# Merge stage in program order: where the norms' activation table is asked for, how wide the late norms work, and which engine makes the first weight sums

## Chip, cores and metric

The kernel runs on one core of one Trainium2 chip. The metric is device time in microseconds for one execution. The kernel before takes 3202.3 us, the median of three runs from 3200.66 to 3202.62 us.

Engines are called by their names in the profile: PE is TensorE (matmuls; PEld are its weight loads), DVE is VectorE, ACT is ScalarE, POOL is GpSimd, and SP is the engine whose queue issues most DMAs.

## What is computed

One encoder layer over 2048 prompt tokens and 32 new tokens, width 1024, in fp32. Cut to what matters here:

```python
h = rmsnorm(x, g_pre_mix) * (1 + scale_m) + shift_m
z = h @ w_in                                    # feeds two mixers and two gates
ya = band_attention(...);  yb = gla(...)
merged = sigmoid(gate_a) * (ya @ w_br_a) + sigmoid(gate_b) * (yb @ w_br_b)
x = x + gate_m * rmsnorm(merged @ w_out, g_post_mix)

h = rmsnorm(x, g_pre_ffn) * (1 + scale_f) + shift_f
u = h @ w_up                                    # 1024 -> 5632
yf = (gelu(conv3(u)[:2816]) * conv3(u)[2816:]) @ w_down
x = x + gate_f * rmsnorm(yf, g_post_ffn)
```

`rmsnorm` needs 1/sqrt(mean(x*x) + eps) for each token.

## The kernel before

**Number format.** Each fp32 factor of a product is split into a high part (an ACT copy that rounds) and a low part (a DVE subtraction), and each product is three matmuls: high by high, high by low, low by high.

**Layout.** Activations lie transposed: channels on the 128 partitions, in eight tiles `m` = 0 to 7, tokens along the row. The 2080 tokens are cut into eight blocks `b` of 260 columns.

**Merge stage (about 1480 to 1781 us of the profile).** For each block four `merge` steps form two tiles each of the merged branches, and eight `project` steps multiply by `w_out`. `begin()` and `end()` bracket a slot, one such step. What the other engines do for a slot is put into a plan by slot and rank (`at(slot, rank, f)`) and written out by `flush`. From line 1218 all five engines are in program order: the order of the text is the order of each queue, so an instruction that waits holds everything behind it on its engine.

**The planned norms.** `norm_plan` does blocks 0 to 5 wholly and the first norm of block 6: thirteen norms. `share` takes the sum of squares (`sa1` after the projection, `sa2` before the feed-forward), splits it (ACT L1317, DVE L1320) and sums it over the partitions with two matmuls by ones (PE L1324, L1325). Two slots on, `rstd_of` makes 1/sqrt: ACT `Ln` (L1332), ACT `Exp` (L1333), and a Newton step of three DVE operations (L1334 to L1336). `ln_exp_table()` (L105) asks for the activation table that holds both functions. It is called at line 1221, where the stage in program order begins, and not in `rstd_of`. The stage's remaining ACT functions are Copy, Square and Identity.

**The late norms.** Blocks 6 and 7 are finished while the feed-forward runs, by the generator `norms(b)`, which starts in the second column of token pair 1 (`hold`). It goes one step further in each `side()`, of which a column has seven. It works by single tiles of 128x260: for each of eight `m` a multiplication, a step later an addition of x, a step later a square, two steps per tile; then the second norm; then for each `m` a multiplication, the shift on ACT a step later, and a store to `h2T` a step later, one step per tile. `rstd_late` calls `ln_exp_table()` itself (L1418). It hands two matmuls to the next column's start and goes on in that column's sixth step.

**Who waits for the late norms.** `ndone` counts blocks whose `h2T` is stored. `sums(2)` builds the operand sums of token pair 2 from `h2T` and stores them in `hT`; it waits for `ndone` = 8. `load_ops` fetches the operands of pair 2 (ACT L1719, DVE L1720) from column 18 of pair 1 on. When both generators have ended, `s3` is closed and its space becomes two more weight buffers and one more place in the ring of split weights.

**Feed-forward.** The products run as seven half-size products in place of eight (a Strassen-like scheme), for three pairs of token segments. `UNITS[0]` to `UNITS[2]` are the up-projection of the three pairs with 22 columns each; one column is seven products of twelve matmuls (L1868). For pair 0 the sums of weight quarters (S1 to S4) are made and stored to `sW`; pairs 1 and 2 read them back. `total3` makes S1, S2, S3 with three operations of 128x512 (L1779): on POOL for unit 0, on DVE for the first units of the down-projection. S4 is on DVE in all of them. The splits of weights are ACT L1805 and DVE L1810, their loads SP L1775, the stores of the sums SP L1813.

Of the kernel before, what the change touches and what calls it, by code (L numbers as in the profile page):

```python
# [13 lines left out]
AF = mybir.ActivationFunctionType  # L14
# [6 lines left out]
KD = 8  # L21
# [10 lines left out]
ND = 260  # L32
# [7 lines left out]
def dap(ap, offset, dims):  # L40
    return bass.AP(tensor=ap.tensor, offset=ap.offset + offset, ap=dims)
# [6 lines left out]
def parts(c0, n):  # L48

    out = []  # L50
    if c0 < TP:
        out.append((0, min(n, TP - c0), 0))
    if c0 + n > TP:
        out.append((max(0, TP - c0), n, 1))
    return out
# [3 lines left out]
def encoder_step(ctx: ExitStack, tc: tile.TileContext, I, O):  # L59
    nc = tc.nc  # L60
# [44 lines left out]
    def ln_exp_table():  # L105
        i = nc.scalar.preload_act_table_set("natural_log_exp_and_others")
        if not in_order[0]:
            tc.keep_in_program_order(i)
# [14 lines left out]
    h2T = dram.tile([D, T], F32, name="h2T")  # L123
# [114 lines left out]
    with ExitStack() as st:  # L238
# [178 lines left out]
        for s_ in range(2, 10):  # L417
            b = s_ // 2
# [799 lines left out]
    ordered.enter_context(tc.manual_schedule(engines={getattr(mybir.EngineType, x) for x in  # L1218
                                                      ("PE", "Activation", "DVE", "Pool", "SP")}))
    in_order[0] = True  # L1220
    ln_exp_table()

    MH = [(area(fA[0], 9232, KD, ND), area(fA[1], 8192, KD, ND)),
          (area(mhl, 0, KD, ND), area(mhl, KD * ND, KD, ND))]
    o_ = [d3.tile([128, KD, ND], F32, name=f"o{x}") for x in range(2)]
    sa1, sa2, sqE, sqR, h2 = [d3.tile([128, 2, ND], F32, name=x) for x in ("sa1", "sa2", "sqE", "sqR", "h2")]
# [3 lines left out]
    def two(dt):  # L1230
        return [d3.tile([128, ND], dt, name=x, tag=x) for x in ("sh", "sl")]
# [15 lines left out]
    def rows2(src, j, b):  # L1247
        return dap(src, 256 * j * T + ND * b, [[T, 128], [128 * T, 2], [1, ND]])
# [62 lines left out]
    def share(b, slot, sa, r):  # L1311
# [15 lines left out]

        after_pe[slot + 1] = total

    def rstd_of(q, r):  # L1330
        r0, t = two(F32)
        nc.scalar.activation(r0, q, AF.Ln, bias=eps, scale=1.0 / D)  # L1332
        nc.scalar.activation(r0, r0, AF.Exp, scale=-0.5)  # L1333
        nc.vector.scalar_tensor_tensor(t, q, D * EPS, r0, op0=OP.add, op1=OP.mult)  # L1334
        nc.vector.scalar_tensor_tensor(t, t, -0.5 / D, r0, op0=OP.mult, op1=OP.mult)
        nc.vector.scalar_tensor_tensor(r, t, 1.5, r0, op0=OP.add, op1=OP.mult)  # L1336
# [3 lines left out]
    def over2(r):  # L1340
        return r.unsqueeze(1).to_broadcast([128, 2, ND])
# [9 lines left out]
    def squares(b, j, s):  # L1351
        nc.scalar.activation(s, o_[b % 2][:, 2 * j:2 * j + 2], AF.Square)

    def x1_store(b, j):
        nc.sync.dma_start(rows2(x1T, j, b), o_[b % 2][:, 2 * j:2 * j + 2])

    def shift(b, x, m):
        for a, e, s in parts(ND * b, ND):
            nc.scalar.activation(x[:, a:e], x[:, a:e], AF.Identity, bias=mod[:, 3, m, s:s + 1],
                                 scale=mod[:, 4, m, s:s + 1])  # L1360
# [86 lines left out]
    def soon(n, f):  # L1447

        later(n - 1, f) if in_order[0] else f()

    def norms(b):

        o, t0, xl = o_[b % 2], ND * b, (h2, sqR)

        def square(m):
            nc.scalar.activation((sa2 if m < 2 else sqE)[:, m % 2], o[:, m], AF.Square)
            if m % 2:
                x1_store(b, m // 2)
                if m > 1:
                    soon(1, lambda: nc.vector.tensor_add(sa2, sa2, sqE))  # L1460

        def add(m):
            nc.vector.tensor_add(o[:, m], o[:, m], xl[m // 2 % 2][:, m % 2])
            soon(1, lambda: square(m))

        def modulate(m):
            nc.vector.tensor_mul(o[:, m], o[:, m], r)

            def store():
                nc.sync.dma_start(h2T[128 * m:128 * m + 128, t0:t0 + ND], o[:, m])  # L1470
                if m == KD - 1:
                    ndone[0] += 1

            def late():
                shift(b, o[:, m], m)
                soon(1, store)

            soon(1, late)

        while hold[0]:  # L1480
            yield
        for j in range(2):
            nc.sync.dma_start(xl[j], rows2(I["xT"], j, b))
        yield
        yield
        r = rs1
        if b == NBLK - 1:
            yield from rstd_late(sa1[:, 0])
        for m in range(KD):
            nc.vector.tensor_mul(o[:, m], o[:, m], r)  # L1490
            soon(1, lambda m=m: add(m))
            yield
            yield
            if m in (1, 3):
                nc.sync.dma_start(xl[m // 2], rows2(I["xT"], 2 + m // 2, b))
        yield
        yield
        pair_sum(sa2)
        yield
        yield  # L1500
        r = yield from rstd_late(sa2[:, 0])
        for m in range(KD):
            modulate(m)
            yield

    NBLK = T // ND
# [1 line left out]
    ndone = [0]  # L1508
# [251 lines left out]
    def weights():  # L1760


        cols = [(u, m) for u in range(len(UNITS)) for m in range(NM[u])]
        fresh = [UNITS[u][0] == 0 for u, m in cols]
        todo = [(c, x) for c in range(len(cols)) for x in (("A21", "A22", "A11", "A12") if fresh[c] else WOPS)]
        at = {}
        born = {}
        cur = -1

        def fetch():  # L1770
            while todo and free and todo[0][0] <= cur + 1:
                c, x = todo.pop(0)
                at[c, x] = i = free.pop(0)
                born[c, x] = tick[0]
                nc.sync.dma_start(raw(i, NK[cols[c][0]]), w_rows(*cols[c], x))  # L1775

        def total(c, eng, op, out, a, b):
            n = NK[cols[c][0]]
            getattr(eng, op)(raw(out, n), raw(a, n), raw(b, n))  # L1779

        def total3(c):
            at[c, "S1"] = s1 = free.pop(0)
            s2, a21 = free.pop(0), at.pop((c, "A21"))
            born.update({(c, x): tick[0] + 1 for x in ("S1", "S2", "S3")})
            eng = nc.vector if cols[c][0] else nc.gpsimd
            a11, a22 = at[c, "A11"], at[c, "A22"]
            total(c, eng, "tensor_add", s1, a21, a22)

            def others():
                total(c, eng, "tensor_sub", s2, s1, a11)  # L1790
                total(c, eng, "tensor_sub", a21, a11, a21)
                at[c, "S2"], at[c, "S3"] = s2, a21

            soon(1, others)

        def part(c, x, i):
            u, m = cols[c]
            while True:
                place = ring((u, m, x))
                if place:  # L1800
                    break
                yield
            n = NK[u]
            hi, lo = place
            act = nc.scalar.activation(hi[:, :n], raw(i, n), AF.Copy)  # L1805
            if not in_order[0]:
                tc.keep_in_program_order(act)

            def low():
                nc.vector.tensor_sub(lo[:, :n], raw(i, n), f32(hi[:, :n]))  # L1810
                WO[u, m, x] = place
                if fresh[c] and x in SUM:
                    nc.sync.dma_start(w_rows(u, m, x), raw(i, n))  # L1813
                if fresh[c] and x == "A12":

                    def total4():
                        total(c, nc.vector, "tensor_sub", i, i, at[c, "S2"])
                        at[c, "S4"] = i

                    soon(1, total4)  # L1820
                elif fresh[c] and x == "S2":
                    soon(4, lambda: free.append(at.pop((c, "S2"))))
                else:
                    soon(3 if fresh[c] and x in SUM else 1, lambda: free.append(i))

            soon(1, low)

        fetch()
        yield
        for cur in range(len(cols)):  # L1830
            for x in SPLITS if fresh[cur] else WOPS:
                if fresh[cur] and (cur, "S1") not in at and x == SPLITS[0]:
                    while len(free) < 2:
                        yield
                    total3(cur)
                if x == "A22" and cur + 1 < len(cols) and fresh[cur + 1] and len(free) > 1 \
                        and all((cur + 1, y) in at for y in ("A21", "A22", "A11")):
                    total3(cur + 1)
                while (cur, x) not in at:
                    fetch()  # L1840
                    if (cur, x) not in at:
                        yield
                while in_order[0] and cur < 5 and tick[0] < born.get((cur, x), -9) + 2:

                    yield
                i = at[cur, x]
                if not (fresh[cur] and x == "S2"):
                    del at[cur, x]
                yield from part(cur, x, i)
                yield  # L1850
                fetch()
# [471 lines left out]
```

## Time and profile before

| | |
|---|---|
| profiled execution | 3196.12 us |
| its span | 3194.4 us |
| median of three runs | 3202.3 us |
| PE busy | 3066.6 us (96%) |
| DVE busy | 2240.5 us (70%) |
| ACT busy | 1682.3 us (53%) |
| POOL busy | 373.5 us (12%) |
| mean TensorE clock granted | 0.988 |

A group's row in the profile gives line, engine, operation, tiles written and read, shape, count, then busy time and mean duration in ns, then the idle time of the engine just before and what ended it. In rows in order of time the first number is the start in us, the second the duration, and the bracket holds the engine's idle time before and the releaser. Rows of windows give the busy time and the number of instructions of each engine, the granted clock, the DMA share and GB/s. Rows of waits give total us, number of times, longest.

### The profile page before, as it was taken

What the parts mean: (1) busy time and instruction counts of PE and PEld (TensorE: products, weight loads), DVE (VectorE), ACT (ScalarE), POOL (GpSimd) and SP (SyncE); (2) the same over time, 40 slices, a digit from 0 to 9 for tenths busy, and PEclk for the clock granted to TensorE, in tenths of its full rate; (3) what the DMA queues carried; (4) which work ended last, traced back from release to release, by engine and by line L of the source; (5) the groups of instructions that cost most, each with busy time, mean ns of one, the idle gap of its engine ahead of it and who ended that gap; (6) DMA issues with size and microseconds to landing.
All of it is one profiled execution on the core that took longest, in us unless ns stands there. A gap on an engine that the chain in (4) does not pass through costs nothing. (4 is left out here: it accounts for less than half of the span.)

```text
span 3194.4 us, 56613 instructions
## 1 busy us (share of the span) xinstructions
PE 3066.6 (96%) x19748; PEld 2949.6 (92%) x19748; DVE 2240.5 (70%) x4861; ACT 1682.3 (53%) x3826; POOL 373.5 (12%) x483
## 2 busy tenths in 40 slices
PE   6999999999999999999999899999999999999997
PEld 4899999998999999888998899999999999999997
DVE  6735517774555555566667799898978778897877
ACT  5412224443555555544565655567756556676755
POOL 2102201111111111110000233300000000000001
PEclk8999999999999999999999999999999999999998
DMA  7344435545433333575456676787897667888784
GB/s 224 99 144 130 141 106 135 141 128 136 117 108 108 107 101 110 175 215 183 143 179 201 194 246 212 233 255 219 228 271 218 190 191 222 266 248 284 236 269 148
DMA packets 598927, 580.13 MB, mean 182 GB/s; under 512 B 53329, under 2 KB 527138, under 8 KB 598642
## 3 DMA queue, kind: packets, MB, share of 16 engines
q1 hardware_dynamic: 553954, 528.92, 55.3%
q10 hardware_dynamic: 44432, 47.34, 4.6%
q8 instruction: 155, 2.54, 0.3%
q14 instruction: 130, 1.06, 0.1%
q0 software_dynamic: 256, 0.26, 0.0%
HBM read 388.71 MB, written 187.65 MB: 180 GB/s over the span
## 5 line engine op out<-in xcount | busy, mean ns | idle before, releaser
L1868 PE MATMUL ad<-hA,hB 128*128 128x350 f32 (+2 forms) x1752 | 303.3, 323 | 1.6 <-ACT work L1994 1.4
L78 PE MATMUL pm<-hA,wh 128*128 128x416 f32 x768 | 290.1, 378 | 0.0
L1868 PEld LDWEIGHTS ad<-hA,hB 128*128 128x128 f32 x1752 | 285.3, 189 | 2.3 <-ACT work L1994 1.7
L80 PE MATMUL pm<-hA,wl 128*128 128x416 f32 x768 | 269.9, 351 | 0.0
L79 PE MATMUL pm<-hA,wh 128*128 128x416 f32 x768 | 269.9, 351 | 0.0
L1810 DVE TENSOR_TENSOR hA<-raws,hA 128x512 fp32r<-128x512 f32 (+1 forms) x368 | 251.0, 689 | 16.1 <-ACT hA L1805 16.1
L1805 ACT ACTIVATE hA<-raws 128x512 fp32r<-128x512 f32 (+1 forms) x368 | 224.3, 617 | 34.8 <-DMA raws<-in_w_up_dram 13.4
L1868 PE MATMUL ad<-hA 128*128 128x348 f32 (+2 forms) x1287 | 225.6, 325 | 7.3 <-DVE hA L1720 3.3
L1868 PEld LDWEIGHTS ad<-hA 128*128 128x128 f32 x1287 | 210.4, 190 | 9.7 <-ACT work L1994 4.5
L1868 PE MATMUL ad<-hA,hA 128*128 128x348 f32 (+2 forms) x1245 | 213.8, 323 | 1.3 <-ACT work L1994 0.6
L1868 PE MATMUL g<-hA,hB 128*128 128x350 f32 (+2 forms) x1143 | 199.7, 323 | 8.1 <-DVE hA L1720 4.4
L1810 DVE TENSOR_TENSOR hB<-raws,hB 128x512 fp32r<-128x512 f32 (+1 forms) x288 | 199.8, 701 | 8.4 <-ACT hB L1805 8.2
L1868 PEld LDWEIGHTS ad<-hA,hA 128*128 128x128 f32 x1245 | 201.5, 188 | 2.3 <-ACT work L1994 0.9
L1868 PEld LDWEIGHTS g<-hA,hB 128*128 128x128 f32 x1143 | 185.3, 188 | 10.8 <-DVE hA L1720 5.2
L1805 ACT ACTIVATE hB<-raws 128x512 fp32r<-128x512 f32 (+1 forms) x288 | 175.2, 618 | 23.1 <-DMA raws<-in_w_up_dram 13.1
L69 ACT ACTIVATE pth<-pp 128x256 fp32r<-128x256 f32 (+1 forms) x288 | 106.3, 375 | 145.0 <-PE pp L1023 136.5
L78 PE MATMUL pn<-wh,hA 128*128 128x256 f32 (+1 forms) x624 | 176.9, 283 | 0.0
L79 PE MATMUL pn<-wl,hA 128*128 128x256 f32 (+1 forms) x624 | 176.3, 283 | 0.0
L80 PE MATMUL pn<-wh,hA 128*128 128x256 f32 (+1 forms) x624 | 176.1, 282 | 0.0
L1977 ACT COPY g<-ad 128x348 f32<-128x348 f32 (+2 forms) x102 | 44.3, 434 | 238.2 <-PE ad L1868 162.9
L934 POOL TENSOR_SCALAR P<-P,mx 128x640 f32<-128x640 f32 (+5 forms) x136 | 104.5, 768 | 530.7 <-DVE mx L933 191.5
L72 DVE TENSOR_TENSOR ptl<-pp,pth 128x256 fp32r<-128x256 f32 (+1 forms) x288 | 117.5, 413 | 63.7 <-ACT pth L69 60.9
(509 smaller groups left out, 8671.7 us busy)
## 6 DMA issues: line engine op xcount, KB each, us to landing
raws<-in_w_up_dram SPq DMA_DIRECT2D x220, 256.0 KB, 4.1
raws<-sW SPq DMA_DIRECT2D x176, 256.0 KB, 3.9
sW<-raws SPq DMA_DIRECT2D x88, 256.0 KB, 3.6
raws<-in_w_down_dram SPq DMA_DIRECT2D x80, 256.0 KB, 4.7
wr<-in_w_in_dram SPq DMA_DIRECT2D x76, 256.0 KB, 3.2
sgT<-tx ACTq DMA_DIRECT2D x80, 208.0 KB, 2.6
wa<-in_w_ada_dram SPq DMA_DIRECT2D x64, 256.0 KB, 2.9
keys<-ks SPq DMA_DIRECT2D x128, 128.0 KB, 2.9
```

Of the source, the lines that this page charges most:

```text
L69: i = nc.scalar.activation(hi, src, AF.Copy)
L72: nc.vector.tensor_sub(lo, src, f32(hi))
L78: nc.tensor.matmul(out, ah, bh, start=first and i == 0, stop=False)
L79: nc.tensor.matmul(out, ah, bl, start=False, stop=False)
L80: nc.tensor.matmul(out, al, bh, start=False, stop=last and i == n - 1)
L934: nc.gpsimd.tensor_scalar(P[:m, :tot], P[:m, :tot], mx[:m, 6:7], 1.0, op0=OP.mult, op1=OP.mult)
L1805: act = nc.scalar.activation(hi[:, :n], raw(i, n), AF.Copy)
L1810: nc.vector.tensor_sub(lo[:, :n], raw(i, n), f32(hi[:, :n]))
L1868: nc.tensor.matmul(out[:, :w], l_[:, k], r_[:, k, :w], start=first and k == 0 and i == 0, stop=k == n - 1 and i == 2, skip_group_check=True)
L1977: nc.scalar.copy(g[:, 0, :w], ad[:, 0, :w])
```

## The change

Three edits. (1) The request for the table moves from the start of the stage to just before the first `Ln` in `rstd_of`. (2) `norms` works by pairs of tiles (128x520): four multiplications, additions, squares, two steps per pair; four multiplications before the shift, two steps per pair, the shift still by tile, and one store per pair. (3) `total3` makes its sums on DVE for unit 0 too.

```diff
@@ stage in program order @@
     in_order[0] = True
-    ln_exp_table()
...
+    tabled = []
+
     def rstd_of(q, r):
         r0, t = two(F32)
+        if not ndone[0] and not tabled:
+            tabled.append(1)
+            ln_exp_table()
         nc.scalar.activation(r0, q, AF.Ln, bias=eps, scale=1.0 / D)
@@ norms(b) @@
-        def square(m):
-            nc.scalar.activation((sa2 if m < 2 else sqE)[:, m % 2], o[:, m], AF.Square)
-            if m % 2:
-                x1_store(b, m // 2)
-                if m > 1:
-                    soon(1, lambda: nc.vector.tensor_add(sa2, sa2, sqE))
+        def pair(j):
+            return o[:, 2 * j:2 * j + 2]
+
+        def square(j):
+            squares(b, j, sqE if j else sa2)
+            x1_store(b, j)
+            if j:
+                soon(1, lambda: nc.vector.tensor_add(sa2, sa2, sqE))
...
-                nc.sync.dma_start(h2T[128 * m:128 * m + 128, t0:t0 + ND], o[:, m])
-                if m == KD - 1:
+                nc.sync.dma_start(rows2(h2T, j, b), pair(j))
+                if j == 3:
                     ndone[0] += 1
...
-        for m in range(KD):
-            nc.vector.tensor_mul(o[:, m], o[:, m], r)
-            soon(1, lambda m=m: add(m))
+        for j in range(4):
+            nc.vector.tensor_mul(pair(j), pair(j), over2(r))
+            soon(1, lambda j=j: add(j))
             yield
             yield
-            if m in (1, 3):
-                nc.sync.dma_start(xl[m // 2], rows2(I["xT"], 2 + m // 2, b))
+            if j < 2:
+                nc.sync.dma_start(xl[j], rows2(I["xT"], 2 + j, b))
...
-        for m in range(KD):
-            modulate(m)
+        for j in range(4):
+            modulate(j)
+            yield
             yield
@@ total3(c) @@
-            eng = nc.vector if cols[c][0] else nc.gpsimd
+            eng = nc.vector
```

More of the change, by code (lines that the diff above doesn't have):

```diff
@@ L1451, in norms, with add, modulate @@
     def norms(b):
-        o, t0, xl = o_[b % 2], ND * b, (h2, sqR)
-        def square(m):
-            nc.scalar.activation((sa2 if m < 2 else sqE)[:, m % 2], o[:, m], AF.Square)
-            if m % 2:
-                x1_store(b, m // 2)
-                if m > 1:
-                    soon(1, lambda: nc.vector.tensor_add(sa2, sa2, sqE))
[L1462 to L1466, printed above, removed]
-            nc.vector.tensor_mul(o[:, m], o[:, m], r)
+        o, xl = o_[b % 2], (h2, sqR)
+        def pair(j):
[5 more added lines that the diff above has]
+                soon(1, lambda: nc.vector.tensor_add(sa2, sa2, sqE))
+        def add(j):
+            nc.vector.tensor_add(pair(j), pair(j), xl[j % 2])
+            soon(1, lambda: square(j))
+        def modulate(j):
+            nc.vector.tensor_mul(pair(j), pair(j), over2(r))
             def store():
-                nc.sync.dma_start(h2T[128 * m:128 * m + 128, t0:t0 + ND], o[:, m])
-                if m == KD - 1:
+                nc.sync.dma_start(rows2(h2T, j, b), pair(j))
+                if j == 3:
                     ndone[0] += 1
             def late():
-                shift(b, o[:, m], m)
+                for i in range(2):
+                    shift(b, o[:, 2 * j + i], 2 * j + i)
                 soon(1, store)
@@ L1488, in norms @@
             yield from rstd_late(sa1[:, 0])
-        for m in range(KD):
-            nc.vector.tensor_mul(o[:, m], o[:, m], r)
-            soon(1, lambda m=m: add(m))
+        for j in range(4):
+            nc.vector.tensor_mul(pair(j), pair(j), over2(r))
+            soon(1, lambda j=j: add(j))
             yield
             yield
-            if m in (1, 3):
-                nc.sync.dma_start(xl[m // 2], rows2(I["xT"], 2 + m // 2, b))
+            if j < 2:
+                nc.sync.dma_start(xl[j], rows2(I["xT"], 2 + j, b))
         yield
```

## The prediction

> **What bounds the kernel now.** I read the page first, then the stage in windows, then PE's gaps in order of time, then the waits around each gap. From the page:
>
> ```profile
> PE 3066.6 (96%) x19748; PEld 2949.6 (92%) x19748; DVE 2240.5 (70%) x4861; ACT 1682.3 (53%) x3826; POOL 373.5 (12%) x483
> ```
>
> PE is busy for 96% of the span, so an engine that is relieved pays only where PE stands still or runs at a lower clock. The windows show where that is (us, then PE, PEld, DVE, ACT, POOL busy, granted clock, DMA):
>
> ```profile
> 1503.00:1770.00 267.00, 255.28 (x2080) 253.10 (x2081) 173.45 (x284) 152.01 (x289) 5.12 (x12) 0.99 0.54 166
> 1770.00:1810.00 40.00, 32.39 (x204) 30.18 (x203) 30.85 (x38) 25.93 (x55) 9.12 (x10) 0.91 0.71 224
> 1810.00:1925.00 115.00, 110.58 (x672) 109.26 (x671) 104.97 (x149) 61.28 (x105) 34.94 (x22) 0.99 0.73 235
> 1925.00:2100.00 175.00, 175.00 (x1089) 174.75 (x1088) 159.95 (x225) 102.48 (x177) 62.92 (x36) 1.00 0.73 230
> 2100.00:2300.00 200.00, 197.72 (x1231) 196.31 (x1230) 180.98 (x310) 139.94 (x255) 0.40 (x4) 1.00 0.78 223
> 2300.00:2400.00 100.00, 92.77 (x568) 92.18 (x567) 81.22 (x131) 53.90 (x93) 0.40 (x4) 0.97 0.93 270
> ```
>
> PE idles 11.7 us in the merge stage, 7.6 in the turn to the feed-forward, 4.4 in the first pair, 2.3 while the late norms run, and 7.2 just behind them: 33 us in reach of the three edits. The large gaps:
>
> ```profile
> 1712.08 0.39 PE L1324 MATMUL pst<-sh,ones 128*128 128x260 f32 x1 [4.76 <-ACT sh L1317]
> 1762.41 0.39 PE L1324 MATMUL pst<-sh,ones 128*128 128x260 f32 x1 [2.91 <-ACT sh L1317]
> 1797.16 3.28 PE L1868 MATMUL ad<-hA 128*128 128x350 f32 x10 [3.32 <-DVE hA L1720]
> 1866.21 3.67 PE L1868 MATMUL g<-hA,hA 128*128 128x350 f32 x12 [2.10 <-ACT g L1977]
> 2365.86 2.21 PE L1868 MATMUL g<-hA 128*128 128x348 f32 x12 [1.82 <-ACT work L1990]
> 2381.14 3.85 PE L1868 MATMUL g<-hB,hA 128*128 128x348 f32 x12 [5.41 <-ACT g L1977]
> ```
>
> A gap costs more than its length. Behind three of them the clock was
>
> ```profile
> 1712.00:1716.00 4.00, 3.85 (x17) 3.65 (x18) 3.05 (x6) 2.14 (x5) 0.00 (x0) 0.57 0.90 229
> 1866.00:1870.00 4.00, 3.79 (x14) 3.79 (x15) 4.00 (x3) 1.61 (x4) 3.92 (x3) 0.57 0.65 220
> 2381.00:2385.00 4.00, 3.85 (x13) 3.86 (x14) 4.00 (x8) 1.99 (x4) 0.00 (x0) 0.51 1.08 359
> ```
>
> 0.57, 0.57 and 0.51 for 4 us: 1.7, 1.7 and 2.0 us of work lost beside the gap. I charge 1.7 us to each gap above 2 us.
>
> The Trainium skill (TensorE: Matmul & The Clock Gate, Part 1: The HAM clock gate) has the clock halve after an idle window of about 3.4 us. The trace does not agree: a gap of 2.10 us was followed by 0.57. By the page the gap of 2.91 us would lose no clock, and the sum below would be 1.7 us smaller.
>
> **Edit 1, the table.** ACT's groups for `Ln`, `Exp` and the requested loads, and then one norm in order of time:
>
> ```profile
> L1332 ACT ACT_TABLE_LOAD x13 | 16.7, 1283 | 0.2
> L1333 ACT ACT_TABLE_LOAD x13 | 16.7, 1283 | 0.2
> L106 ACT ACT_TABLE_LOAD x9 | 11.5, 1283 | 1.8 <-ACT nx L536 0.9 <-PEq L2304 0.8
> ```
>
> ```profile
> 1684.74 1.28 ACT L1333 ACT_TABLE_LOAD   x1
> ...
> 1764.63 0.39 ACT L1302 ACTIVATE sa<-po 128x260 f32<-128x260 f32 x1
> 1765.03 1.28 ACT L1332 ACT_TABLE_LOAD   x1
> 1766.82 1.28 ACT L1333 ACT_TABLE_LOAD   x1
> 1768.57 0.43 DVE L1334 SCALAR_TENSOR_TENSOR sl<-pst,sh 128x260 f32<-128x260 f32 x1 [5.14 <-ACT sh L1333]
> ```
>
> Each of the thirteen planned norms loads a table before `Ln` and another before `Exp`, although line 1221 asked for one that holds both. That request has nothing to wait for and was evidently carried to the front of ACT's queue, where other functions replace it; the late norms, which ask right before their `Ln`, show no load at their own lines. Put behind earlier instructions of the stage, the request should stay there. Then 26 loads become one: 25 x 1.283 = 32 us less on ACT. What it is worth is decided by who waits:
>
> ```profile
> DVE sl L1334 <- ACT sh L1333: 55.3, 13, 6.6
> PE pst L1324 <- ACT sh L1317: 8.0, 3, 4.8
> PE pst L1325 <- DVE sl L1320: 3.0, 4, 1.2
> ```
>
> DVE stands 55.3 us in 13 waits for `Exp`; two loads, 2.57 us, are in each, so 33 of the 55 go. Behind the waiting DVE instruction stand the sums and splits of the next norm, and PE waits for those at L1324 and L1325, 11.0 us in all. I read three parts. The four waits at L1325, and 0.34 us left over at L1324, come soon after a table pair: each is at most 1.2 us, below the 2.57 that goes: 3.3 us. The wait of 2.91 us at 1762 follows a pair too, and also POOL's first sums (edit 3): 2.9 + 1.7 of clock = 4.6 us. The wait of 4.76 us at 1712 is not so near one: the last load ended at 1686, 21 us before that gap begins, and in between DVE also waits for stores and loads of `h2T`. It can gain 0 to 6.5 us from a stage that runs less late; I take 3, near the half. Sum 10.9 us, bounds 4 to 15. PE's work hides the remainder of the 32 us.
>
> The Trainium skill (ScalarE: Activation LUTs, What ACT_TABLE_LOAD costs) adds a drain of about 1380 ns to each load, 2.66 us a switch. The rows do not show it: the load begins 0.01 us after the square ends. By the page 25 loads would free 67 us of ACT instead of 32; the sum would hardly move, since PE's gaps cap it.
>
> **Edit 3, the first pair's sums.** The rows of POOL and DVE (windows 1740 to 2110, 1810 to 2100, 2100 to 2300), with two single DVE additions and the longest class of POOL's waits on a store:
>
> ```profile
> L1779 POOL TENSOR_TENSOR raws<-raws 128x512 f32<-128x512 f32 x66 | 111.1, 1697 | 215.2 <-DVE hB L1810 62.4 <-DVE hA L1810 43.7 <-DMA sW<-raws 39.4
> L1779 DVE TENSOR_TENSOR raws<-raws 128x512 f32<-128x512 f32 x20 | 13.6, 680 | 0.0
> L1810 DVE TENSOR_TENSOR hA<-raws,hA 128x512 fp32r<-128x512 f32 x76 | 58.9, 790 | 5.8 <-ACT hA L1805 5.7
> L1810 DVE TENSOR_TENSOR hB<-raws,hB 128x512 fp32r<-128x512 f32 x68 | 53.6, 804 | 1.3 <-ACT hB L1805 1.3
> L1810 DVE TENSOR_TENSOR hA<-raws,hA 128x512 fp32r<-128x512 f32 x60 | 40.6, 682 | 3.3 <-ACT hA L1805 3.3
> ```
>
> ```profile
> 1758.66 1.77 DVE L1306 TENSOR_TENSOR sa<-sa,sqE 128x520 f32<-128x520 f32 x1
> 1773.75 0.69 DVE L1306 TENSOR_TENSOR sa<-sa,sqE 128x520 f32<-128x520 f32 x1
> ```
>
> ```profile
> POOL raws L1779 <- DMA sW<-raws: 39.4, 4, 10.3
> ```
>
> DVE gets 66 operations of 0.680 us, 45 us. It loses POOL's interference: the same addition took 1.77 us beside POOL and 0.69 without, and 144 splits averaged about 797 ns with POOL at work against 682 after it, 16.5 us; other two-operand operations add to this, so DVE's net load rises by 28 us at most. Its idle time from 1770 to 2100 is 9.2 + 10.0 + 15.1 = 34 us. It fits, closely: DVE is near full from here on, and after the merge stage every spare microsecond counts. For the gain: the gaps at 1762 (counted above) and 1797 follow stretched DVE operations, and POOL's lateness no longer holds weight buffers. For the loss: from 1810 to 1925 DVE already has 105 of 115 us. PE's gaps and clock losses here are 7.6 + 4.4 + 2 x 1.7 = 15 us. Bounds: +10 (most of that) to -11 (45 us of load, no relief, less 34 of idle). I take +3, for a turn that gets shorter and a pair that stays as it is.
>
> **Edit 2, late norms by pairs.** From the first step after the release to the last store I count in the code 93 steps before: per norm 16 steps for the additions and 8 for the modulation, and each of the three `rstd_late` waits for a sixth step of a column. By pairs the additions take 8, and with the waits I get 78. A column is 84 matmuls, seven steps; 1231 matmuls in 200 us give 13.65 us, 1.95 us a step. So the end comes 15 steps, 29 us, earlier. What hangs on it:
>
> ```profile
> 2293.94 0.67 SPq L1470 DMA_DIRECT2D h2T<-o  x1
> 2294.65 1.21 SPq L1527 DMA_DIRECT2D ht<-h2T  x1
> 2365.76 1.16 SPq L1558 DMA_DIRECT2D hT<-ht  x2
> SPq L1674 <- DMA hT<-ht: 7.1, 1, 7.1
> 2377.73 0.79 ACT L1719 ACTIVATE hA<-ht 128x700 fp32r<-128x700 f32 x1 [9.71 <-DMA ht<-hT]
> ```
>
> `sums(2)` begins with the last store at 2294 and ends at 2367. SP then stands 7.1 us at the load of those sums, with the weight loads behind it, and ACT 9.7 us at their split, with the weight splits and the copy L1977 behind it: that is PE's gap of 5.41 us. 29 us earlier the sums end near 2338, well before column 18 asks for them. I take 8 of 7.2 + 2.0 us, bounds 2 to 9. DVE's own work falls a little (24 wide operations for 48 narrow ones), but in half the steps; and the second pair of loads of x now has three steps, 5.9 us, where it had five. The first loads already have three, and nothing in the rows of waits shows DVE at them. I cost both at nothing, hidden by a PE that is busy 198 of 200 us there; uncovered, a late load would cost about 1 us each time, four times.
>
> **Sum.** 10.9 + 3 + 8 = 21.9 us. The profiled execution of 3196.1 us becomes 3174; the median of the runs lies 6.2 us above that execution, so 3180 us. This case alone spans 3168 to 3192.
>
> **Rivals.** (a) *DMA sets the gaps.* The stage's slots hide the table, the gap at 1712 stays, the first pair gains nothing and some late wait takes the place of the one at 2381: 3.3 + 0 + 5 = 8 us, 3194. For it: the causes at 1712 and 1866 include transfers. Against: the waits that follow table pairs. 0.14. (b) *DVE waits at its own sums.* S1 goes into a buffer whose store may still run; POOL met that four times, 39.4 us in all, harmlessly, as nothing stood behind it. On DVE the weight splits stand behind. With all 39.4 us and the net 28 us against 34 of idle, the pair loses 34 us: 10.9 + 8 - 34 = -15, 3217 us. It decides from 25 us of such waits on. Against: a store was issued three steps, 5.9 us, before its buffer is handed on. 0.10. (c) *The table is loaded as before*, the request carried off again: 4.6 of the first term goes with POOL, the other terms stay, 12 to 15 us, 3188. 0.04. (d) *More*: nearly all gaps close, 34 us, 3168 and below. 0.06. My forecast has 0.66.
>
> **Numbers.** About 0.2%, 6.4 us, is what a measurement can tell from no change. Faster by more: 0.66 + 0.06 + 0.04 and half of (a), rounded, 0.84. Within: half of (a) and the edge of (b), 0.08. Slower: most of (b) and ill luck in the later order, 0.08. The range runs from 3165 to 3197; it leaves out (b) and the best of (d).
>
> **What would show it.** Right: one table load in the stage, none at L1332 or L1333; DVE's wait at L1334 near 22 us; L1324 and L1325 waiting under 5 us; no POOL sums after 1740; splits at 0.68 us; no gap above 2 us at the end of pair 1, and `sums(2)` ending 25 to 30 us earlier relative to column 0. Wrong: DVE idle ahead of L1779 for a DMA, or PE's idle time from 1810 to 2100 above 10 us, or 26 loads still there.

## The result and the profile after

The kernel after takes 3175.6 us, the median of four runs (3174.99 to 3179.95), against 3201.5 us for the kernel before, four runs (3200.19 to 3202.62). The ratio is 0.9922 with a 95% interval of 0.9905 to 0.9939: faster by 25.9 us, where 3180 us had been forecast from 3202.3. The line numbers of the kernel after differ from those of before, from one lower (L1324 becomes L1323) to eight higher.

The page after, and ACT's loads that were requested by hand:

```profile
PE 3056.5 (96%) x19748; PEld 2942.5 (93%) x19748; DVE 2243.6 (71%) x4903; ACT 1649.5 (52%) x3792; POOL 263.7 (8%) x417
```

```profile
L106 ACT ACT_TABLE_LOAD x9 | 11.5, 1283 | 1.0 <-ACT nx L536 0.9
```

PE runs the same 19748 matmuls and is busy for 10 us less, ACT for 32.8 us less, POOL for 110 us less. No loads are left at the lines of `Ln` and `Exp`. L106 has nine loads before and nine after. In the kernel before, one of them stands at the start of the program, with the load of another function right behind it:

```profile
0.81 1.28 ACT L106 ACT_TABLE_LOAD   x1 [0.81 <-PEq L2304]
2.10 1.28 ACT L103 ACT_TABLE_LOAD   x1
```

The kernel after has none there, and one more in the merge stage: the request of the stage was indeed carried to the front. The first planned norm after, in order of time, shows the load that is left, and `Exp` right behind `Ln`:

```profile
1540.98 1.28 ACT L106 ACT_TABLE_LOAD   x1
1542.28 0.48 ACT L1336 ACTIVATE sh<-pst,eps 128x260 f32<-128x260 f32 x1
1542.79 0.42 ACT L1337 ACTIVATE sh<-sh 128x260 f32<-128x260 f32 x1
```

The waits of the merge stage after (total, times, longest):

```profile
DVE sl L1338 <- ACT sh L1337: 29.6, 12, 5.3
PE pst L1324 <- DVE sl L1319: 1.4, 1, 1.4
PE pst L1323 <- ACT sh L1316: 0.4, 1, 0.4
```

DVE's wait for `Exp` fell from 55.3 to 29.6 us, PE's waits for the norms from 11.0 to 1.8. The end of pair 1, where SP stood 7.1 us and PE 5.41:

```profile
2318.42 1.45 SPq L1566 DMA_DIRECT2D hT<-ht  x2
2331.81 1.92 SPq L1535 DMA_DIRECT2D ht<-h2T  x4
2333.78 0.43 SPq L1682 DMA_DIRECT2D ht<-hT  x1
```

The last sums of pair 2 are stored at 2318, and the first load of them is at 2334. Column 22 is the first of pair 1. Its copy before, and after with the last store of the norms:

```profile
2098.73 0.43 ACT L1977 COPY g<-ad 128x348 f32<-128x348 f32 x1 [1.68 <-PE ad L1868]
```

```profile
2085.06 0.43 ACT L1985 COPY g<-ad 128x348 f32<-128x348 f32 x1 [0.93 <-PE ad L1876]
2253.32 0.37 SPq L1476 DMA_DIRECT2D h2T<-o  x1
```

Counted from that copy, the norms end 27 us earlier than before (168.3 us behind it, not 195.2) and the sums 34 us earlier (233.4, not 267.0). Windows of the kernel after, of 100 us there and of the first pair:

```profile
2300.00:2400.00 100.00, 100.00 (x627) 100.00 (x626) 88.56 (x138) 63.60 (x109) 0.26 (x4) 1.00 0.89 263
1810.00:1925.00 115.00, 110.12 (x682) 109.25 (x681) 108.70 (x178) 59.76 (x104) 0.00 (x0) 1.00 0.76 240
```

PE has no idle time from 2300 to 2400. In the first pair, which begins 12 us earlier than in the kernel before, it still loses 5 us, and DVE is busy for 108.7 of 115 us.

**Where the time came from.** Windows of two kernels do not hold the same work. So I cut each trace at the starts of two ACT operations that every kernel has in the same order: the copy of the merged branch (L1279 before), whose first start opens the merge stage, and the copy in each feed-forward column (L1977 before), of which there are 102. Times between them, in us:

```
                  merge    pair 0   columns   columns
                  to col 0 0 to 22  22 to 43  43 to 101
before            295.6    314.3    296.0     766.2
after             281.7    312.5    288.5     766.2
full_again        281.9    315.0    288.6     768.6
e1_table          282.1    317.3    297.0     766.6
e2_pairs          294.3    314.6    288.3     765.7
e3_sums           293.3    314.3    297.0     767.7
e4_table_pairs    281.5    313.2    288.1     769.0
e4_again          281.5    316.9    288.1     766.6
e5_table_sums     282.2    313.3    297.1     768.2
e6_load_each      285.3    315.5    288.5     767.4
e7_sums2_held     281.3    313.7    298.0     768.4
e8_pool_noise     282.0    323.4    289.4     767.1
e9_square_later   281.3    314.5    288.4     766.0
e11_three_steps   280.9    313.6    288.6     767.9
```

The change gains 13.9 us in the merge stage, 1.8 in pair 0, 7.5 from column 22 to 43, 23 us in all; behind column 43 nothing changes in this trace. The first and the third column repeat within 1.5 us wherever the code there is the same; the second spreads over 4 us, the fourth over 3. The merge stage itself begins anywhere from 1488.8 to 1499.5 us in these traces, in code that no edit touches, so single spans can't be compared by microseconds.

### The profile page after: what moved, and what is told of

Read it like the earlier page. It is cut to its first block, busy times and chain, and to the rows that moved or that the text cites. A ratio compares the mean times of both kernels' runs of the same rounds, so it can differ in the third digit from the quotient of the medians.

```text
span 3173.3 us, 56451 instructions
## 1 busy us (share of the span) xinstructions
PE 3056.5 (96%) x19748; PEld 2942.5 (93%) x19748; DVE 2243.6 (71%) x4903; ACT 1649.5 (52%) x3792; POOL 263.7 (8%) x417
## 5 line engine op out<-in xcount | busy, mean ns | idle before, releaser
L1876 PEld LDWEIGHTS ad<-hA,hB 128*128 128x128 f32 x1734 | 281.7, 189 | 7.3 <-ACT work L2002 3.8
L1818 DVE TENSOR_TENSOR hA<-raws,hA 128x512 fp32r<-128x512 f32 (+1 forms) x367 | 242.0, 668 | 12.5 <-ACT hA L1813 12.2
L1876 PE MATMUL ad<-hA,hA 128*128 128x348 f32 (+2 forms) x1308 | 226.9, 324 | 3.0 <-ACT work L2002 2.2
L1876 PE MATMUL g<-hA,hB 128*128 128x348 f32 (+2 forms) x1248 | 217.2, 323 | 6.7 <-ACT work L1998 3.9
L1876 PEld LDWEIGHTS ad<-hA,hA 128*128 128x128 f32 x1308 | 213.1, 190 | 4.3 <-ACT work L2002 2.8
L1876 PEld LDWEIGHTS g<-hA,hB 128*128 128x128 f32 x1248 | 202.4, 188 | 9.4 <-ACT work L1998 5.0
L1876 PE MATMUL ad<-hA 128*128 128x350 f32 (+2 forms) x1173 | 204.9, 324 | 4.2 <-DVE hA L1728 4.1
L1876 PEld LDWEIGHTS ad<-hA 128*128 128x128 f32 x1173 | 191.5, 190 | 5.0 <-DVE hA L1728 4.4
L1818 DVE TENSOR_TENSOR hB<-raws,hB 128x512 fp32r<-128x512 f32 (+1 forms) x289 | 191.0, 668 | 6.7 <-ACT hB L1813 6.3
L1876 PE MATMUL g<-hA,hA 128*128 128x350 f32 (+2 forms) x894 | 156.1, 323 | 3.3 <-ACT g L1985 1.7
```

The source lines that it names most:

```text
L1876: nc.tensor.matmul(out[:, :w], l_[:, k], r_[:, k, :w], start=first and k == 0 and i == 0, stop=k == n - 1 and i == 2, skip_group_check=True)
```

## The experiments

My theory: the three edits act in three places, through VectorE's wait for `Exp`, through the time at which the sums of pair 2 end, and a little through POOL's interference. Rivals: POOL's interference was the whole price; transfers made the gaps; the extra buffers, not the time, closed the gap at the end of pair 1; VectorE becomes full. Each ratio is to runs of the kernel before that were made beside it, with medians from 3202.7 to 3206.0 us.

**Edit 1 alone.**

```diff
     in_order[0] = True
-    ln_exp_table()
...
+        if not ndone[0] and not tabled:
+            tabled.append(1)
+            ln_exp_table()
```

> Edit 1 alone: one table request before the first Ln, nothing else. My theory: the loads stand in VectorE's way and through it in TensorE's; the merge stage gets 8 to 12 us shorter, the waits at L1324 and L1325 fall below 4 us, and the gap at 1762 shrinks but stays, since POOL's first sums are still there. Rival (the slots hide the table; transfers and POOL make the gaps): under 3 us, and the gap of 4.8 us near 1712 stays.

Ratio 0.9962 (0.9950 to 0.9973). The merge stage is 13.5 us shorter, above the 8 to 12 expected. PE's gaps in the trace:

```profile
1711.23 0.39 PE L1323 MATMUL pst<-sh,ones 128*128 128x260 f32 x1 [0.82 <-ACT sh L1316]
1722.45 0.39 PE L1324 MATMUL pst<-sl,ones 128*128 128x260 f32 x1 [1.65 <-DVE sl L1319]
```

The first is where 4.76 us stood; where the gap at 1762 was there is none, though POOL still makes the sums, and I had expected it to stay. So the table alone made both gaps possible, and the rival of transfers falls. Pair 0 is 3 us longer than before, with the same code: that is the spread named above.

**Edit 2 alone.** All of `norms`, nothing else:

```diff
-        for m in range(KD):
-            nc.vector.tensor_mul(o[:, m], o[:, m], r)
+        for j in range(4):
+            nc.vector.tensor_mul(pair(j), pair(j), over2(r))
...
```

> Edit 2 alone: late norms by pairs. My theory: the sums of pair 2 end 25 to 30 us earlier, the gap of 5.4 us at the end of pair 1 goes, 6 to 8 us in all, after a loss of about 2 us while the norms run. Rival (the gap comes from transfers that are crowded there anyway): a gap of 3 us or more stays at the end of pair 1, gain under 3 us.

Ratio 0.9973 (0.9962 to 0.9984). Columns 22 to 43 take 288.3 us, as in the full change. Columns 22 to 41 alone take 261.4 us against 259.6, a loss of 1.8 us while the norms run; columns 41 to 43 take 26.9 against 36.3.

**Edit 3 alone.**

```diff
-            eng = nc.vector if cols[c][0] else nc.gpsimd
+            eng = nc.vector
```

> Edit 3 alone: S1 to S3 of the first pair on VectorE. My theory: 3 to 7 us faster, most of it before column 1, since the gap at 1762 loses POOL's share; the pair itself stays as it is. Rival (VectorE is full, or waits at its own sums): the pair gets 5 us or more longer and the kernel is no faster.

Ratio 0.9990 (0.9977 to 1.0003): the median is 2 us lower, below the 3 to 7 expected, and no change is not excluded. The merge stage gains 2.3 us on the kernel before, but only 1.0 on the run of edit 2, where its code is that of before; pair 0 gains nothing. The trace shows that the gap of 2.91 us fell to 0.75, and that the gap of over 4 us, now 5.2, did not:

```profile
PE pst L1324 <- ACT sh L1317: 6.5, 4, 5.2
PE pst L1325 <- DVE sl L1320: 3.6, 4, 1.6
```

```profile
1770.62 0.39 PE L1324 MATMUL pst<-sh,ones 128*128 128x260 f32 x1 [0.75 <-ACT sh L1317]
```

The run of edit 2 has 1.44 us there with the code of before, so the fall from 2.91 overstates what edit 3 does.

**Edits 1 and 2, twice.** Against the kernel after:

```diff
-            eng = nc.vector
+            eng = nc.vector if cols[c][0] else nc.gpsimd
```

POOL makes the first sums again. The second time the full change ran beside it.

> Edits 1 and 2, POOL still makes the first sums. My theory: the gains of edits 1 and 2 alone add up, 15 to 20 us, and what is missing from the full change is 3 to 6 us. Rival (edit 3 gives most of the gain, by ending POOL's interference): under 10 us.

> The full change once more, beside the next kernel on the same chip. Ratio to the kernel before 0.990 to 0.994.

> Edits 1 and 2 once more. If edit 3 pays by itself, this is 3 to 6 us slower than the full change. If the table's edit had already closed the gaps that POOL had a share in, within 2 us; the stages of the earlier two traces speak for this (merge 281.5 and 281.8 us, first pair 313.3 and 312.5).

Ratios 0.9936 (0.9918 to 0.9954) and 0.9935 (0.9923 to 0.9946); the full change beside the second, 0.9933 (0.9921 to 0.9945). The medians are 23.2 and 19.9 us below those of before, where 15 to 20 had been expected of edits 1 and 2. So edit 3 adds nothing that can be measured once the table is mended; the intervals leave room for some 4 us either way. The merge stage is 281.5 us without it and 281.7 with it; pair 0 takes 313.2 and 316.9 us without, 312.5 and 315.0 with. The gap at 1762 needed both a late VectorE and POOL: edit 1 alone closes it, edit 3 alone leaves 0.75 us of it.

**Edits 1 and 3.** Against the kernel after, the late norms by tiles:

```diff
-        for j in range(4):
-            nc.vector.tensor_mul(pair(j), pair(j), over2(r))
+        for m in range(KD):
+            nc.vector.tensor_mul(o[:, m], o[:, m], r)
...
```

> Edits 1 and 3, late norms by tiles: the merge stage and the first pair as in the full change, the gap of some 9 us at the end of pair 1 back, 7 to 9 us slower than the full change. If edits 2 and 3 hang together, the first pair differs from the full change's 312.5 us by more than 3.

Ratio 0.9955 (0.9942 to 0.9967). Columns 22 to 43 are back at 297.1 us, 8.6 us longer; the other stages stay. The edits don't hang together.

**A load before every `Ln`.**

```diff
-        if not ndone[0] and not tabled:
-            tabled.append(1)
-            ln_exp_table()
+        ln_exp_table()
```

> The full change with the request before every Ln: thirteen loads where the change has one and the kernel before 26. If the price is VectorE's wait and part of it is slack, half of the loads cost less than half of the merge stage's gain: 0 to 4 us slower than the full change, 3175 to 3180. Rival (each load's time comes through whole): 12 x 1.28 = 15 us slower. Second rival (the merge stage gained by POOL's absence, not by the table): no slower at all.

Ratio 0.9937 (0.9922 to 0.9951). The merge stage is 3.6 us longer than with one load. DVE's wait for `Exp`, and PE's behind it:

```profile
DVE sl L1334 <- ACT sh L1333: 41.8, 13, 5.3
PE pst L1323 <- ACT sh L1316: 2.6, 1, 2.6
PE pst L1324 <- DVE sl L1319: 0.5, 1, 0.5
```

Edit 3 alone, this run and the full change have the same first sums and 26, 13 and 1 load. DVE's wait for `Exp` is 55.3, 41.8 and 29.6 us, and the stage 293.3, 285.3 and 281.7 us. The price rises faster than the dose: of the 15.4 us of the first 12 loads 3.6 come through, of the 16.7 us of the next 13 loads 8.0.

**The sums of pair 2 held back.**

```diff
-                sumq.extend([(NBLK - 2, sums(1)), (NBLK, sums(2))])
+                def held():
+                    for _ in range(15):
+                        yield
+                    yield from sums(2)
+
+                sumq.extend([(NBLK - 2, sums(1)), (NBLK, held())])
```

> The full change with the sums of pair 2 held back by 15 steps, 29 us; the earlier end of the norms and the earlier extra buffers stay. My theory: the gap of about 5 us at the end of pair 1 is back and the kernel is 7 to 10 us slower than the full change. Rival (the extra buffers closed the gap): within 2 us of the full change.

Ratio 0.9958 (0.9944 to 0.9973). The gap is back, in the same chain as in the kernel before. PE, SP and ACT between 2340 and 2400:

```profile
PE g L1876 <- ACT g L1985: 5.5, 1, 5.5
SPq L1682 <- DMA hT<-ht: 6.8, 1, 6.8
ACT hA L1727 <- DMA ht<-hT: 11.0, 2, 9.8
```

Columns 41 to 43 take 36.4 us. The norms ended early and the extra buffers were there; neither helped. The time of the sums is the cause.

**Work on POOL that nothing needs.** After each of VectorE's sums in unit 0, POOL subtracts on a scratch tile; the first of each group reads the sum, so that it comes at that time.

```diff
+            for i in range(0 if cols[c][0] else 4):
+                q = noise if i else raw(s1)[:, 0]
+                nc.gpsimd.tensor_sub(noise, q, q)
...
+                for i in range(0 if cols[c][0] else 8):
+                    q = noise if i else raw(s2)[:, 0]
+                    nc.gpsimd.tensor_sub(noise, q, q)
```

> The full change with added work on POOL that nothing needs: after each of VectorE's first-pair sums as many elements again are subtracted on a scratch tile (128x128, four times for each sum). My theory (POOL's operations stretch VectorE's two-operand ones, and VectorE has some 5% to spare): splits rise from 0.68 to about 0.75 us or more, VectorE is overfull, the first pair gets 5 to 20 us longer. Rival (the stretch lies in slack, as before the change): within 3 us of the full change.

Ratio 0.9954 (0.9938 to 0.9971). Pair 0 takes 323.4 us, 11 more than in the full change and 8 more than in the longest trace with VectorE's sums and no noise. DVE's groups from 1820 to 2090, first of the full change, then with the noise:

```profile
L1818 DVE TENSOR_TENSOR hA<-raws,hA 128x512 fp32r<-128x512 f32 x73 | 48.9, 683 | 2.1 <-ACT hA L1813 2.1
L1787 DVE TENSOR_TENSOR raws<-raws 128x512 f32<-128x512 f32 x73 | 48.3, 681 | 0.0
L1818 DVE TENSOR_TENSOR hB<-raws,hB 128x512 fp32r<-128x512 f32 x64 | 42.9, 683 | 0.5 <-ACT hB L1813 0.5
L1893 DVE SCALAR_TENSOR_TENSOR work<-ad,cw,work 128x696 f32<-128x696 f32 x38 | 35.5, 936 | 0.6
```

```profile
L1789 DVE TENSOR_TENSOR raws<-raws 128x512 f32<-128x512 f32 x73 | 53.3, 749 | 0.0
L1826 DVE TENSOR_TENSOR hA<-raws,hA 128x512 fp32r<-128x512 f32 x70 | 51.1, 746 | 0.8 <-ACT hA L1821 0.8
L1826 DVE TENSOR_TENSOR hB<-raws,hB 128x512 fp32r<-128x512 f32 x61 | 47.0, 783 | 0.0
L1901 DVE SCALAR_TENSOR_TENSOR work<-ad,cw,work 128x696 f32<-128x696 f32 x36 | 33.5, 931 | 0.0
```

Splits go from 683 to 746 and 783 ns, sums from 681 to 749. The noise kept POOL busy longer than the true sums did (135 us against 98 in a window of this length), so 11 us is an upper reading. It shows both halves of the trade of edit 3: the interference is real, and VectorE's room in pair 0 is gone once it makes the sums.

**The late squares a step later.**

```diff
-            soon(1, lambda: square(j))
+            soon(2, lambda: square(j))
```

> The full change with each square of the late norms two steps behind its addition, not one. The trace of the change shows ScalarE waiting up to 3.1 us for the addition, which a full VectorE makes late, and TensorE losing some 2 us while the norms run. If that wait is the cause, 1 to 2 us come back, 3174; if the loss is VectorE's own load, nothing changes.

Ratio 0.9922 (0.9907 to 0.9937), and columns 22 to 41 take 261.5 us, as in the full change: no gain. ACT's wait is not gone but has moved, in the full change and here:

```profile
ACT sqE L1356 <- DVE o L1469: 4.5, 2, 3.1
```

```profile
ACT sqE L1356 <- DVE sa L1466: 4.8, 2, 2.6
```

The square now waits for the addition that frees its buffer, which sits in the same full queue. So this run does not tell ACT's wait from VectorE's load, and I leave that open.

**Three steps for each pair of the additions.**

```diff
             soon(1, lambda j=j: add(j))
             yield
             yield
+            yield
```

> The full change with three steps, not two, for each pair of the late norms' additions: 8 of the 15 steps are given back, the sums of pair 2 end 14 us earlier than in the kernel before, not 29. The sums then end near 2353 on the clock of the kernel before, where column 18 asks for them from 2356 on: the gap at the end of pair 1 should stay away or be under 2 us, and the 2 us lost while the norms run should shrink to about 1. If all 29 us are needed, 4 us or more of the gap are back.

Ratio 0.9929 (0.9916 to 0.9942). Columns 22 to 41 take 260.4 us, a loss of 0.8 and not 2.0; columns 41 to 43 take 28.1 and not 26.9. Both sizes came as expected, and they cancel. The norms end 15 us earlier than in the kernel before, where the full change has 27, and the sums 21 us earlier, where it has 34. That is nearly enough, and no gain was found in this trade. No version that I tried beats the change by more than the measurement can tell.

## Why the prediction was right, and which sizes were off

**The table, forecast 10.9 us, measured 13.9.** The mechanism was right: the 26 loads at `Ln` and `Exp` go and one stands ahead of the first `Ln`, DVE waits less, PE follows. To size the three parts I cut the stage at equal work: 1570 matmuls from the first merge copy to just behind the wait at 1680.9, 300 around the gap at 1712, and 434 that take in the gap at 1762 and end just ahead of column 0. Windows before, then after (each also counts the matmuls at its edges):

```profile
1488.81:1681.93 193.12, 190.24 (x1573) 188.69 (x1572) 124.56 (x203) 107.26 (x203) 0.10 (x1) 1.00 0.53 166
1681.93:1726.35 44.42, 38.34 (x302) 37.73 (x302) 30.56 (x53) 23.90 (x46) 0.54 (x6) 0.96 0.69 211
1726.35:1783.95 57.60, 54.62 (x437) 54.04 (x435) 38.64 (x58) 39.62 (x83) 4.62 (x7) 0.97 0.59 181
```

```profile
1490.82:1680.97 190.15, 188.91 (x1572) 188.36 (x1571) 125.69 (x203) 90.40 (x190) 0.00 (x0) 1.00 0.54 170
1680.97:1719.66 38.69, 36.82 (x302) 36.21 (x301) 30.75 (x53) 18.31 (x42) 0.63 (x7) 1.00 0.78 238
1719.66:1772.13 52.47, 52.47 (x436) 52.47 (x435) 38.06 (x62) 32.50 (x77) 0.26 (x4) 1.00 0.69 213
```

The small waits gave 3.0 us, where 3.3 had been taken, and the gap at 1762 gave 5.1, where 4.6 had been taken. The term that was mis-sized is the gap at 1712: taken at 3, because no load stood close ahead of it, it gave 5.7, near its upper bound of 6.5. With edit 1 alone 0.82 us of its 4.76 are left. That the lateness builds up over several norms, and shows where a transfer uses up the last slack, fits this but is only argued. The charge of 1.7 us of clock for a gap held: in the third stretch the idle time falls by 3.0 us and the stretch by 5.1, with the clock at 1.00 and not 0.97.

In the first stretch the idle time falls by only 1.6 of the 3.0 us. The rest was hidden in matmuls that count as busy. PE in the kernel before, in order of time:

```profile
1572.37 0.28 PE L80 MATMUL po<-hA,hB 128*128 128x260 f32 x1
1572.49 0.28 PE L1324 MATMUL pst<-sh,ones 128*128 128x260 f32 x1
1572.87 0.39 PE L1325 MATMUL pst<-sl,ones 128*128 128x260 f32 x1
```

Matmuls start 0.12 us apart, but each lasts 0.28. The last one starts 0.38 us behind the one before it, 0.26 late, and only 0.10 us of that lies behind the end of the other; the row carries no idle bracket. The count of matmuls in a window tells it. From 1540 to 1620 there are

```profile
1540.00:1620.00 80.00, 79.54 (x661) 79.12 (x661) 54.22 (x90) 49.13 (x93) 0.00 (x0) 1.00 0.48 148
```

in the kernel before, and after

```profile
1540.00:1620.00 80.00, 80.00 (x670) 80.00 (x669) 55.37 (x91) 40.54 (x86) 0.00 (x0) 1.00 0.48 148
```

661 matmuls before and 670 after: nine at 0.12 us are 1.1 us, where the idle time says 0.46.

DVE's wait for `Exp` fell by 25.7 us and not by 33. That DVE reaches the wait earlier once the tables are gone would explain the difference; no run tests it.

**The first pair, forecast +3, measured +1.8 and -0.7 in the two traces of the full change.** The direction can't be told from the spread: five traces with POOL's sums take 313.2 to 316.9 us, eight with VectorE's and no noise 312.5 to 315.5. The step that failed is the credit to edit 3: its share of the gap at 1762 was real only as long as the table was there. A shorter turn was right: behind column 0 the five have gaps of 1.1 and 3.3 us, and four of them one of 1.6; the eight have a single gap of 4.1 us. A pair that stays as it is was not: some 67 us behind column 0 the eight have a gap of 1.3 us that none of the five has. In the full change PE waits there for a split on DVE:

```profile
1838.59 1.24 PE L1876 MATMUL g<-hA,hB 128*128 128x350 f32 x6 [1.34 <-DVE hB L1818]
```

The bound on VectorE's load held: it fits, and the noise run shows how closely. The rival in which VectorE waits at its own sums is refuted: the group L1787 has 0.0 us of idle time ahead of it from 1820 to 2090, and 0.1 from 1740 to 2110.

**The late norms, forecast 8, measured 7.5.** The norms end 27 us earlier where 15 steps were counted as 29, the chain through SP and ACT was the right one, and holding the sums back restores it. The sums end 35 us earlier counted from column 0, more than the 25 to 30 named as a sign: before, their last quarter took 23 us and not 18 like the two ahead of it, and after it takes 17. Why it was slow is open. The cost of doing the norms in more work per step was taken as nothing, with PE's 198 of 200 us as cover; it is 2.0 us against the trace of before, and 1.0 to 2.1 over all traces (259.6 to 260.2 us by tiles, 261.2 to 261.7 by pairs, without the noise and the third step). The gain at the end is 9.5, all of the 9.2 that was there.

**The whole, forecast 21.9, measured 25.9 in the medians.** The errors of the three parts cancel in part, which is luck: the table gave 3.0 us more, the pair 1.2 and the norms 0.5 less. From the merge stage to the last column it is 23 us in the trace of the change and 18 in its second trace, where pair 0 and the last columns were 5 us longer. The offset of 6.2 us between the profiled execution and the median was carried over; it belonged to that one execution. The profiled execution after took 3174.99 us, only 0.6 below the median of its runs. In the second comparison the full change gained 22.9 us of medians.

The drain that the Trainium skill (ScalarE: Activation LUTs, What ACT_TABLE_LOAD costs) adds to a table load had no part: in the trace after too, `Ln` starts 0.02 us after the load ends.

## What to carry to other kernels

A request for a table must stand behind the instructions that it has to follow, right at its first user; look in the trace for loads at the users' own lines before believing that one request was enough. Where PE seems busy, count matmuls per microsecond against a clean stretch, since waits shorter than a matmul's pipelined length do not show as idle. And when two delays meet in one gap, remove each alone before giving both a price: here the second edit to close it was worth nothing that could be measured.

## What was not expected of the hardware

The same delay at 1, 13 and 26 places cost 0, 3.6 and 11.5 us: part of it is hidden in the slack of the schedule, and the first half more than the second. DVE's operations that read `ad` from PSUM kept their time beside POOL's noise (L1901, 931 ns, against 936 without), while sums and splits with two operands in SBUF went from 681 and 683 to as much as 783 ns. Not all such operations did: the 128x696 products (L1933) took 869 ns beside the noise, 873 without, and 1107 in the kernel before beside POOL's sums. What decides it was not tested.
